# RWKV chunks as affine maps of the state

## The chip, the cores and the metric

The kernel runs on one core of one Trainium2 chip. The metric is the device time of one execution in microseconds (us), lower is better. A core has a matrix engine (TensorE, PE in the views, with its weight loads as PEld), a vector engine (VectorE, DVE), a scalar engine (ScalarE, ACT), GpSimd (POOL) and SyncE (SP), which issues transfers. Each engine works through its own list of instructions in order and waits at an instruction until what that needs is there.

## What is computed

One inference step of a hybrid layer, for a prompt of 512 tokens and 8 x 4 sample tokens, in fp32. The input projection feeds an HGRN2 branch (a, 4 heads of 128) and an RWKV-7 branch (b, 8 heads of 64); both are projected out, merged by gates and followed by an MLP. The change lies in the RWKV branch of the prompt, whose state S (64 x 64 for each head) goes from token to token:

```python
def step(S, xs):
    rt, wt, kt, vt, kkt, at = xs
    sk = jnp.einsum('bhij,bhj->bhi', S, kkt)
    S = S * wt[:, :, None, :] - sk[..., None] * (kkt * at)[:, :, None, :] + vt[..., None] * kt[:, :, None, :]
    return S, jnp.einsum('bhij,bhj->bhi', S, rt)
...
S, y = lax.scan(step, s0.astype(f32), (tr(r), tr(w), tr(k), tr(v), tr(kk), tr(a)))
...
u = jnp.einsum('btd,dc->btc', h, w_in)
o_a, s_a_new = _hgrn2_branch(u_a, lb, hgrn_norm_w, s_a)
o_b, s_b_new = _rwkv7_branch(u_b, u_b_prev, s_b, ...)
x = x + (gate_a * (o_a @ w_a_out) + gate_b * (o_b @ w_b_out)) @ w_out
x = x + jnp.square(jax.nn.relu(rmsnorm(x) @ w_up)) @ w_down
```

## The kernel before

**GEMM.** Every large product is made of three fp32r products (high x high, low x high, high x low). `split` (L166) takes a loaded weight tile `st` apart: ScalarE writes the high part `whi`, VectorE the rest `wlo`. `in_unit` (L410) makes 128 columns of the input projection in two halves of 24 matmuls, `half_unit` (L1345) the same for the branches' output projections, which come after the recurrences: first branch b, then branch a. `branch` (L1350) loads a branch's output from memory (`ox`) and makes its high and low parts `oh` and `ol`, one pair for each of four heads or head pairs.

**Lanes.** The recurrences are generators. A string `ORDER` lists the units of the input projection and, between them, what is put on either of two lanes; after each unit `pump` takes so many steps from lane X and so many from lane Y, by the rate written in the string (`=25` is 2 of X and 5 of Y). What is not done when the units are through goes on beside the output projection of branch b (`NPB` steps of lane Y for each of its units). Lane X holds both RWKV groups (`rw_all(0)`, `rw_all(1)`) and HGRN head 3 (marked `x`), lane Y the other heads, the state and the sample work; the last one on lane Y is `hg2`, head 2. Lane X has three PSUM banks: two of `pe` and one of `pr`, each handed on when its reader is done. A scheduler of the framework then sets the final order of each engine, and mixes the steps with the GEMM matmuls.

**RWKV.** A group g holds two pairs of heads, and a pair fills the 128 rows. The 512 tokens are 8 chunks of 64. `rw_batch` makes for every chunk the decayed keys and queries (`KR`: part 0 the keys that meet the state, part 1 the queries), and masked products between them (`Az`, `Ar`, from `rw_batch_pa`). `rw_inverse` and `rw_solve` make the inverse matrix `TTp` of every chunk; `rw_values` and `rw_tokens` turn values (`VU`, upper half) and keys (`BE`) round and make `av`. `later_pairs` makes the decays of pairs 2 and 3 and sends them to memory (`sa_d`).

`rw_chain` (L762) then walks the chunks. For each of them TensorE multiplies the state with the keys (`pz`), VectorE makes `z` from it (`ch`, L138, two instructions), TensorE applies the inverse (`pu`, written `rw_chain_pq<-ch,TT`), VectorE copies the result beside the values (`VU`, L788), TensorE makes the new state (`ps`, `rw_chain_pq<-VU,BE`), and VectorE scales it and adds the decayed old one (`st`, L138). The chunk's output `py` is two more products in the same step. So a chunk goes three times from TensorE to VectorE and back. `rw_out` norms the output and turns it round with `swapped` (16 matmuls with the identity, `rw_out_pt`).

Of the kernel before, what the change touches and what calls it, by code (L numbers as in the profile page):

```python
# [60 lines left out]
def hybrid_step(ctx: ExitStack, tc: tile.TileContext, i, o):  # L61
# [438 lines left out]
    bv, zb, Az, Ar, chan, VU, av, BE, yo = ({} for _ in range(9))  # L500
# [25 lines left out]

    def later_pairs():
        for p in (2, 3):
            x = [S(TOK, name="sa") for _ in range(2)]
            decay_and_a(p, *x)  # L530
            for e in range(2):
                nc.sync.dma_start(out=sa_d[:, p - 2, e, :], in_=x[e])
            yield
# [15 lines left out]
    def rw_batch(pairs, xk, xr, xv):  # L549
# [16 lines left out]
        for q, p in enumerate(pairs):  # L566
# [39 lines left out]
            for h in range(2):  # L606
                Az[p, h], Ar[p, h] = (S(512, name="A").rearrange("p (n w) -> p n w", w=64) for _ in range(2))
            for e in range(2):
# [39 lines left out]
    def rw_tokens(p):  # L648
# [6 lines left out]
        for j in range(2):  # L655
            if not e:
                av[g, j] = S(512, name="av").rearrange("p (n e w) -> p n e w", n=4, e=2)
            act(av[g, j][:, :, e, :], pav[:, 4 * j:4 * j + 4, :])
        yield
        for j in range(2):  # L660
# [3 lines left out]
            BE[p, j] = S(512, name="BE").rearrange("p (n h w) -> p n h w", n=4, h=2)  # L664
            act(BE[p, j].rearrange("p n h w -> p (n h w)"), pt)
# [95 lines left out]

    def rw_chain(g):  # L762
# [3 lines left out]
        py_ = pe("rw_chain_py").rearrange("p e (n w) -> p e n w", w=64)  # L766
        ST = {p: S(512, name="st").rearrange("p (n w) -> p n w", w=64) for p in pairs}
        tmp = S(384, name="ch")
        z = tmp[:, 0:256].rearrange("p (e h w) -> p e h w", e=2, h=2)
        dec = tmp[:, 256:384].rearrange("p (e w) -> p e w", e=2)  # L770
        P.memset(z, 0.0)
        for n in range(8):
            pq = pr("rw_chain_pq")
            pz, ps = (pq[:, 128 * j:128 * j + 128].rearrange("p (e w) -> p e w", e=2) for j in range(2))
            pu = pq[64:128, 256:512].rearrange("p (e w) -> p e w", e=2)
            vu = VU[g, n // 2][:, n % 2]
            if n:
                for e, p in enumerate(pairs):
                    for r in hs:
                        mm(pz[r, e, :], KR[p][r, 0, n, :], ST[p][r, n - 1, :])  # L780
            for h, r in enumerate(hs):
                if n:
                    stt(z[r, :, h], pz[r], -1.0, av[g, n // 4][r, n % 4], ALU.mult, ALU.subtract)
                else:
                    tsc(z[r, :, h], av[g, 0][r, 0], -1.0, ALU.mult)
            for e, p in enumerate(pairs):
                mm(pu[:, e], TTp[p][:, n, :], z[:, e].rearrange("p h w -> p (h w)"))
            V.tensor_copy(out=vu[64:128].rearrange("p e h w -> p e (h w)"), in_=pu)  # L788
            for e, p in enumerate(pairs):
                for h, r in enumerate(hs):  # L790
                    mm(ps[r, e, :], BE[p, n // 4][:, n % 4, h, :], vu[:, e, h, :])
            for e, p in enumerate(pairs):
                s = pcs[:, p, n:n + 1]
                if n:
                    stt(ST[p][:, n, :], ps[:, e, :], s, dec[:, e, :], ALU.mult, ALU.add)
                else:
                    tsc(ST[p][:, n, :], ps[:, e, :], s, ALU.mult)
                if n < 7:
                    tsc(dec[:, e, :], ST[p][:, n, :], pcs[:, p, n + 1:n + 2], ALU.mult, 1.0, ALU.mult, eng=P)
            for e, p in enumerate(pairs):  # L800
# [486 lines left out]
    for tok in ORDER.split():  # L1287
# [17 lines left out]
        n = int(n)  # L1305
# [308 lines left out]
```

## Time and profile before

| | |
|---|---|
| median of 3 executions | 1004.47 us (998.51, 1004.47, 1006.31) |
| profiled execution | 998.07 us, of it span 996.4 us |
| TensorE busy | 949.0 us (95%) |
| its weight loads | 900.5 us (90%) |
| VectorE busy | 585.7 us (59%) |
| ScalarE busy | 392.8 us (39%) |
| GpSimd busy | 132.4 us (13%) |
| chain 1 (group 0) / chain 2 (group 1) | 193.9 to 231.9 us / 362.7 to 405.4 us |

The span runs from the first to the last instruction of the profiled execution; 1.67 us of its time lie outside. A matmul's row in the timeline is a group of like matmuls: its start, the time from the first one's start to the last one's end, line, tile written and tiles read, and how many records (an fp32 matmul of small tiles leaves two records, a GEMM matmul one). Matmuls overlap, so the price of a group is read as the distance from its start to the next group's. The number in square brackets at a row's end is the time the engine stood idle before it, with what it waited for.

### The profile page before, as it was taken

Reading aid. Unit: us, or ns where it says so; the run is one execution under the profiler, and the core shown is the slowest. Engines: PE = TensorE matmul, PEld = TensorE weight load, DVE = VectorE, ACT = ScalarE, POOL = GpSimd, SP = SyncE. Lnnn points to the kernel's source line nnn. Section 1 sums busy time; section 2 is a strip of 40 time slices with the busy share of each in tenths; the row PEclk is TensorE's granted clock in tenths of the full one; section 3 lists DMA queues with packets and bytes.
Section 4 is the critical chain, followed back from the end, with each engine's and each line's share of the span. In section 5 each row is a group of like instructions: output and inputs, shape, how many; then the busy total and the mean of one; then the engine's idle time right before and its main releaser. Section 6 shows DMA issues by size and latency. Waiting matters only on the chain.

```text
span 996.4 us, 21381 instructions
## 1 busy us (share of the span) xinstructions
PE 949.0 (95%) x8900; PEld 900.5 (90%) x8900; DVE 585.7 (59%) x1198; ACT 392.8 (39%) x721; POOL 132.4 (13%) x330
## 2 busy tenths in 40 slices
PE   5999998899998899898999999999999999999996
PEld 5999888889987876787899999999999999999995
DVE  6645979578886944698778554444222244445333
ACT  7554545514636431434444333333111233333232
POOL 4486332122222001101000000000000000000000
PEclk9999999999999999999999999999999999999998
DMA  9532343222534132553743642223223332335111
GB/s 265 162 120 85 80 91 98 60 65 81 154 100 107 35 95 65 145 163 121 257 127 121 198 127 84 86 85 86 85 86 90 95 92 85 86 106 144 48 43 48
DMA packets 191091, 106.38 MB, mean 107 GB/s; under 512 B 38945, under 2 KB 179047, under 8 KB 190994
## 3 DMA queue, kind: packets, MB, share of 16 engines
q1 hardware_dynamic: 165424, 95.16, 32.8%
q10 hardware_dynamic: 25570, 9.85, 3.9%
q8 instruction: 70, 1.15, 0.5%
q14 instruction: 27, 0.22, 0.1%
HBM read 85.08 MB, written 18.39 MB: 104 GB/s over the span
## 4 chain that ended last, share of the span: by engine, by line
PE 59%; DVE 4%; DMA 1%; ACT 1%; issue 1%; ACTq 0%; SPq 0%; POOL 0%; DVEq 0%
PE pd L129 24%; PE full_unit_ps L129 19%; PE in_unit_ps L129 7%; PE half_unit_ps L129 4%; PE rw_chain_pq L129 1%; DMA s0A<-in_state_hgrn_dram 1%; PE rw_sample_pn L129 1%; PE rw_chain_py L129 1%; DVE wlo L135 1%; DVE tmp L135 0%; PE fin_t L1468 0%; DVE bn L726 0%; DVE ad L1098 0%; PE hg_head_pl L129 0%; ACT jk L132 0%
## 5 line engine op out<-in xcount | busy, mean ns | idle before, releaser
L132 ACT ACTIVATE whi<-st 128x1024 fp32r<-128x1024 f32 x120 | 126.8, 1057 | 252.6 <-PE pd L129 119.2
L135 DVE TENSOR_TENSOR wlo<-st,whi 128x1024 fp32r<-128x1024 f32 x120 | 148.3, 1236 | 124.8 <-PE full_unit_ps L129 40.3
L129 PE MATMUL in_unit_ps<-h_hi,wlo 128*128 128x272 f32 (+3 forms) x736 | 121.5, 299 | 3.5 <-DVE wlo L135 3.5
L129 PE MATMUL in_unit_ps<-h_hi,whi 128*128 128x272 f32 (+3 forms) x736 | 119.2, 297 | 2.4 <-ACT U L132 1.3
L129 PE MATMUL in_unit_ps<-h_lo,whi 128*128 128x272 f32 (+3 forms) x736 | 120.8, 298 | 0.0
L129 PE MATMUL full_unit_ps<-hd,whi 128*128 128x272 f32 (+2 forms) x832 | 110.2, 288 | 0.0
L129 PEld LDWEIGHTS in_unit_ps<-h_hi,wlo 128*128 128x128 f32 x736 | 103.2, 193 | 7.5 <-DVE wlo L135 4.0
L129 PEld LDWEIGHTS in_unit_ps<-h_hi,whi 128*128 128x128 f32 x736 | 101.8, 191 | 7.6 <-issue 3.5
L129 PEld LDWEIGHTS in_unit_ps<-h_lo,whi 128*128 128x128 f32 x736 | 103.4, 193 | 3.7 <-issue 2.1
L129 PEld LDWEIGHTS full_unit_ps<-hd,whi 128*128 128x128 f32 x832 | 106.4, 188 | 0.0
L129 PE MATMUL pd<-xgl,whi 128*128 128x272 f32 x512 | 70.2, 289 | 0.0
L129 PE MATMUL pd<-xgh,wlo 128*128 128x272 f32 x512 | 69.8, 288 | 0.0
L129 PE MATMUL pd<-xgh,whi 128*128 128x272 f32 x512 | 69.8, 288 | 0.0
L129 PEld LDWEIGHTS pd<-xgl,whi 128*128 128x128 f32 x512 | 66.7, 188 | 0.0
L129 PEld LDWEIGHTS pd<-xgh,whi 128*128 128x128 f32 x512 | 66.2, 188 | 0.0
L129 PEld LDWEIGHTS pd<-xgh,wlo 128*128 128x128 f32 x512 | 66.2, 188 | 0.0
L141 POOL TENSOR_SCALAR ys<-ys,ssf 32x512 f32<-32x512 f32 x1 | 0.8, 831 | 491.1 <-DVE ssf L1497 491.1
L129 PE MATMUL full_unit_ps<-hd,wlo 128*128 128x272 f32 (+2 forms) x416 | 56.8, 288 | 0.0
L129 PEld LDWEIGHTS full_unit_ps<-hd,wlo 128*128 128x128 f32 x416 | 54.0, 188 | 0.0
L135 DVE TENSOR_TENSOR hd<-r,hd 128x544 fp32r<-128x544 f32 x32 | 23.2, 725 | 47.9 <-ACT hd L132 47.9
L135 DVE TENSOR_TENSOR x<-x,full_unit_ps 128x272 f32<-128x272 f32 (+2 forms) x48 | 19.5, 435 | 37.0 <-PE full_unit_ps L129 37.0
L138 DVE SCALAR_TENSOR_TENSOR r<-pd,rsb 128x272 f32<-128x272 f32 x64 | 25.2, 436 | 25.8 <-PE pd L129 23.9
(412 smaller groups left out, 1479.8 us busy)
## 6 DMA issues: line engine op xcount, KB each, us to landing
st<-in_w_in_dram SPq DMA_DIRECT2D x46, 512.0 KB
st<-in_w_up_dram SPq DMA_DIRECT2D x32, 512.0 KB
st<-in_w_down_dram SPq DMA_DIRECT2D x32, 512.0 KB
gt_d<-gt SPq DMA_DIRECT2D x16, 272.0 KB
st<-in_w_out_dram SPq DMA_DIRECT2D x8, 512.0 KB
gtb<-gt_d SPq DMA_DIRECT2D x8, 272.0 KB
gta<-gt_d SPq DMA_DIRECT2D x8, 272.0 KB
x<-xt_d SPq DMA_DIRECT2D x8, 272.0 KB
```

What stands on the lines that cost most here:

```text
L129: T.matmul(out, lhsT, rhs, start=start, stop=stop)
L132: A.activation(out=out, in_=in_, func=func, **kw)
L135: (eng or V).tensor_tensor(out=out, in0=a, in1=b, op=op)
L138: V.scalar_tensor_tensor(out=out, in0=a, scalar=s, in1=b, op0=op0, op1=op1)
L141: (eng or V).tensor_scalar(out=out, in0=a, scalar1=s1, scalar2=s2, op0=op0, op1=op1)
```

## The change

`rw_chain` is written anew, and a step `rw_affine` is put ahead of it. With the chunk's inverse known, the new state is (a matrix of the chunk) times the old state plus a constant of the chunk, and the output likewise. `rw_affine` makes these for each pair and each half of the chunks: `pw`, eight products of `TTp` with `KA` (the turned keys beside what was `av`), copied by ScalarE into `W` and, negated, into `VU`; then `pq`, eight products of `W` with `CB` (what was `BE`, beside what was `Ar`), from which VectorE makes `GQ` in two instructions. The chain then has one group of products per chunk (`VU,CB` and `st,GQ` summed in one PSUM tile) and one VectorE instruction, which scales both pairs. The outputs of all chunks are made after the chain, one pair after the other. `rw_tokens` turns the keys round with 16 more small matmuls per pair (`rw_batch_pk`), and its copies write parts of `KA` and `CB`. `later_pairs` becomes a part of `first_pairs`, so that the decays of pairs 2 and 3 are made early, and their four transfers (on SP's queue) stand between the first loads of `w_in`.

The removed lines of `rw_chain` are those printed above and are left out here.

```diff
--- before.py
+++ after.py
@@ -497,7 +497,7 @@
     zb_d = [dram.tile([4, 16, 32, 32], F32, name=f"zb_d{g}") for g in range(2)]
     xz_d = [dram.tile([4, 16, 32, 32], F32, name=f"xz_d{g}") for g in range(2)]
     gb_d = dram.tile([128, 4, TOK], F32, name="gb_d")
-    bv, zb, Az, Ar, chan, VU, av, BE, yo = ({} for _ in range(9))
+    bv, zb, Az, chan, VU, KA, CB, yo = ({} for _ in range(8))
     zero = S(512, name="zero")
     P.memset(zero, 0.0)
     for g in range(2):
@@ -523,8 +523,6 @@
             sig[p], al[p] = S(TOK, name="sig"), S(TOK, name="al")
             decay_and_a(p, sig[p], al[p])
             yield
-
-    def later_pairs():
         for p in (2, 3):
             x = [S(TOK, name="sa") for _ in range(2)]
             decay_and_a(p, *x)
@@ -604,7 +602,7 @@
             yield
 
             for h in range(2):
-                Az[p, h], Ar[p, h] = (S(512, name="A").rearrange("p (n w) -> p n w", w=64) for _ in range(2))
+                Az[p, h] = S(512, name="A").rearrange("p (n w) -> p n w", w=64)
             for e in range(2):
                 pa = pe("rw_batch_pa")
                 for j in range(4):
@@ -612,9 +610,11 @@
                         r = slice(64 * h, 64 * h + 64)
                         mm(pa[:, h, 128 * j:128 * j + 128], eb[e][r, j], KR[p][r, :, 4 * e + j, :])
                 p4 = pa.rearrange("p h (j m w) -> p h j m w", j=4, m=2)
-                for m, dst in enumerate((Az, Ar)):
-                    for h in range(2):
-                        tt(dst[p, h][:, 4 * e:4 * e + 4, :], p4[:, h, :, m], bc(msk[:, m, :], 1, 4), ALU.mult)
+                for h in range(2):
+
+                    CB[p, e, h] = S(512, name="CB").rearrange("p (n w) -> p n w", n=4)
+                    for m, dst in enumerate((Az[p, h][:, 4 * e:4 * e + 4, :], CB[p, e, h][:, :, 64:128])):
+                        tt(dst, p4[:, h, :, m], bc(msk[:, m, :], 1, 4), ALU.mult)
                 yield
             for k in range(4):
                 (nc.sync, DQ)[k % 2].dma_start(
@@ -653,16 +653,20 @@
             for h in range(2):
                 mm(pav[64 * h:64 * h + 64, n, :], Az[p, h][0:64, n, :], VU[g, n // 2][0:64, n % 2, e, h, :])
         for j in range(2):
-            if not e:
-                av[g, j] = S(512, name="av").rearrange("p (n e w) -> p n e w", n=4, e=2)
-            act(av[g, j][:, :, e, :], pav[:, 4 * j:4 * j + 4, :])
+            KA[p, j] = S(512, name="KA").rearrange("p (n w) -> p n w", n=4)
+            act(KA[p, j][:, :, 64:128], pav[:, 4 * j:4 * j + 4, :])
+        yield
+        pt = LX.one("rw_batch_pk")
+        swapped(KR[p][:, 0].rearrange("p n w -> p (n w)"), pt)
+        for j in range(2):
+            act(KA[p, j][:, :, 0:64], pt[:, 256 * j:256 * j + 256].rearrange("p (n w) -> p n w", n=4))
         yield
         for j in range(2):
             pt = LX.one("rw_batch_pt")
             for n in range(4):
                 T.transpose(pt[:, 128 * n:128 * n + 128], chan[p][j][:, n].rearrange("p m w -> p (m w)"), ident)
-            BE[p, j] = S(512, name="BE").rearrange("p (n h w) -> p n h w", n=4, h=2)
-            act(BE[p, j].rearrange("p n h w -> p (n h w)"), pt)
+            for h in range(2):
+                act(CB[p, j, h][:, :, 0:64], pt.rearrange("p (n h w) -> p n h w", n=4, h=2)[:, :, h])
             yield
 
     TTp, Dg = {}, {}
@@ -759,57 +763,64 @@
             act(TTp[p][64 * c:64 * c + 32, :, 32:64], px[64 * c:64 * c + 32])
         yield
 
+    GQ = {}
+
+    def rw_affine(g):
+
+        for e in range(2):
+            p = 2 * g + e
+            for j in range(2):
+                pw = pe("rw_affine_pw").rearrange("p h (n w) -> p h n w", n=4)
+                for n in range(4):
+                    for h in range(2):
+                        r = slice(64 * h, 64 * h + 64)
+                        mm(pw[64:128, h, n], TTp[p][r, 4 * j + n, :], KA[p, j][r, n, :])
+                W = S(512, name="W1").rearrange("p (h n w) -> p h n w", h=2, n=4)
+                act(W[64:128], pw[64:128, :, :, 0:64])
+                for i2 in range(2):
+                    act(VU[g, 2 * j + i2][64:128, :, e].rearrange("p n h w -> p h n w"),
+                        pw[64:128, :, 2 * i2:2 * i2 + 2, 64:128], AF.Copy, scale=-1.0)
+                yield
+                pq = pr("rw_affine_pq").rearrange("p (n w) -> p n w", n=4)
+                for n in range(4):
+                    for h in range(2):
+                        mm(pq[64 * h:64 * h + 64, n], W[64:128, h, n, :], CB[p, j, h][64:128, n, :])
+                GQ[p, j] = S(512, name="GQ").rearrange("p (n w) -> p n w", n=4)
+                tt(GQ[p, j][:, :, 0:64], bc(I2, 1, 4), pq[:, :, 0:64], ALU.subtract)
+                tt(GQ[p, j][:, :, 64:128], KR[p][:, 1, 4 * j:4 * j + 4, :], pq[:, :, 64:128], ALU.subtract)
+                yield
+
     def rw_chain(g):
 
         pairs = (2 * g, 2 * g + 1)
         hs = (slice(0, 64), slice(64, 128))
...
+        ST = [S(512, name="st").rearrange("p (n e w) -> p n e w", n=4, e=2) for _ in range(2)]
         for n in range(8):
...
+            ps = LX.one("rw_chain_ps")[:, 0:128].rearrange("p (e w) -> p e w", e=2)
             vu = VU[g, n // 2][:, n % 2]
+            for e, p in enumerate(pairs):
+                for h, r in enumerate(hs):
+                    mm(ps[r, e, :], CB[p, n // 4, h][:, n % 4, 0:64], vu[:, e, h, :], e == 0, e == 1 and n == 0)
             if n:
                 for e, p in enumerate(pairs):
                     for r in hs:
...
+                        mm(ps[r, e, :], GQ[p, n // 4][r, n % 4, 0:64], ST[(n - 1) // 4][r, (n - 1) % 4, e, :], False, e == 1)
+            tt(ST[n // 4][:, n % 4], ps, bc(pcs[:, 2 * g:2 * g + 2, n], 2, 64), ALU.mult)
+            yield
+        for e, p in enumerate(pairs):
+            py_ = LX.one("rw_chain_py").rearrange("p (n w) -> p n w", w=64)
+            for n in range(8):
                 for h, r in enumerate(hs):
...
+                    mm(py_[r, n, :], CB[p, n // 4, h][:, n % 4, 64:128], VU[g, n // 2][:, n % 2, e, h, :], True, n == 0)
                 if n:
                     for r in hs:
...
+                        mm(py_[r, n, :], GQ[p, n // 4][r, n % 4, 64:128], ST[(n - 1) // 4][r, (n - 1) % 4, e, :], False, True)
+            yo[p] = S(512, name="yo").rearrange("p (n w) -> p n w", w=64)
+            act(yo[p], py_)
+            yield
+        pw_ = LX.one("rw_chain_pw_")[:, 0:256].rearrange("p (q c) -> p q c", q=2)
         for e, p in enumerate(pairs):
-            yo[p] = S(512, name="yo").rearrange("p (n w) -> p n w", w=64)
-            act(yo[p], py_[:, e])
-        pw_ = pr("rw_chain_pw_")[:, 0:256].rearrange("p (q c) -> p q c", q=2)
-        for e, p in enumerate(pairs):
-            T.transpose(pw_[0:64, e, :], ST[p][:, 7, :], ident)
+            T.transpose(pw_[0:64, e, :], ST[1][:, 3, e, :], ident)
         so = S(256, name="so")
         act(so[0:64], pw_[0:64].rearrange("p q c -> p (q c)"))
         DQ.dma_start(out=o["wkv_p"][0, 0, 4 * g:4 * g + 4].rearrange("h v k -> v h k"),
@@ -983,8 +994,6 @@
             yield from rw_values(g)
             for p in pairs:
                 yield from rw_tokens(p)
-            if g == 0:
-                yield from later_pairs()
 
         more = meanwhile()
         for _ in rw_inverse(g):
@@ -994,6 +1003,7 @@
         yield from more
         for p in pairs:
             yield from rw_solve(p)
+        yield from rw_affine(g)
         yield from rw_chain(g)
         for p in pairs:
             yield from rw_out(p)
```

How the instructions stand on TensorE, at three places. First, one chunk of the second chain. Before, in the program's order (`kr` is KR, `TT` the inverse, `rw_sample` the sample tokens' work):

```order
L129 MATMUL rw_chain_pq_4792<-st_4710,kr_3682 64x64 x2
L129 MATMUL rw_chain_pq_4792<-st_4711,kr_3885 64x64 x2
L129 MATMUL rw_sample_pn_5204<-um_5202,rs_4143 64x512
L129 MATMUL in_unit_ps_5244<-h_hi,whi_5240 128x272 x6
L129 MATMUL rw_chain_pq_4792<-ch_4712,TT_4492 64x128
L129 MATMUL rw_chain_pq_4792<-ch_4712,TT_4653 64x128
L129 MATMUL in_unit_ps_5244<-h_hi,whi_5240 128x272 x2
L129 MATMUL in_unit_ps_5244<-h_hi,wlo_5241 128x272 x3
L968 MATMUL rw_sample_pt_5209<-ident,s0T_3918 128x128 x3
L129 MATMUL rw_chain_pq_4792<-VU_4078,BE_4132 64x64 x2
L129 MATMUL rw_chain_pq_4792<-VU_4078,BE_4285 64x64 x2
```

In the change:

```order
L129 MATMUL rw_chain_ps_5164<-st_5041,GQ_4953 64x64 x2
L129 MATMUL rw_chain_ps_5164<-st_5041,GQ_5037 64x64 x2
L129 MATMUL rw_chain_ps_5174<-VU_4316,CB_3934 64x64
L129 MATMUL rw_chain_ps_5174<-VU_4316,CB_3937 64x64
L129 MATMUL rw_chain_ps_5174<-VU_4316,CB_4167 64x64
L129 MATMUL rw_chain_ps_5174<-VU_4316,CB_4170 64x64
L129 MATMUL in_unit_ps_5513<-h_hi,whi_5484 128x272 x2
L129 MATMUL rw_chain_ps_5174<-st_5041,GQ_4953 64x64 x2
L129 MATMUL rw_chain_ps_5174<-st_5041,GQ_5037 64x64 x2
```

The step with the inverse (`ch,TT`) and the VectorE work on either side of it have gone; two matmuls of the GEMM are left between a chunk's constant part (`VU,CB`) and its state part (`st,GQ`), where 6, 2 and 3 stood between the old steps.

Second, what stands ahead of the second chain. Before, the last rows of `rw_solve` and the first of the chain:

```order
L129 MATMUL rw_solve_py_4670<-XT_4650,zb_4050 32x32 x16
L129 MATMUL in_unit_ps_5169<-h_hi,whi_5140 128x272 x6
L129 MATMUL rw_solve_px_4690<-TT_4653,YT_4687 32x32 x16
L129 MATMUL in_unit_ps_5169<-h_hi,wlo_5141 128x272 x6
L129 MATMUL rw_chain_pq_4714<-ch_4712,TT_4492 64x128
L129 MATMUL rw_chain_pq_4714<-ch_4712,TT_4653 64x128
L129 MATMUL in_unit_ps_5169<-h_hi,wlo_5141 128x272 x2
```

In the change, a part of `rw_affine` that stands between them (eight `pq` per pair and half, of which the rows show the last two and the next first two):

```order
L129 MATMUL rw_affine_pq_4944<-CB_3934,W_4930 64x128
L129 MATMUL rw_affine_pq_4944<-CB_3937,W_4930 64x128
L129 MATMUL rw_affine_pw_4966<-KA_4424,TT_4771 64x128 x8
L129 MATMUL in_unit_ps_5320<-h_lo,whi_5291 128x272 x5
L129 MATMUL in_unit_ps_5488<-h_hi,whi_5484 128x272 x2
L129 MATMUL rw_affine_pq_5003<-CB_4140,W_4975 64x128
L129 MATMUL rw_affine_pq_5003<-CB_4143,W_4975 64x128
```

These are new rows: 32 `pw` and 32 `pq` for each group, in runs of eight or sixteen between runs of the GEMM.

Third, the end of the second lane against the start of branch a's output projection. `hg_head_pt<-ident,hy` are head 2's last transposes, `half_unit_ps` the output projections; the `oh` of the first rows are branch b's, and those behind the line of dots branch a's, the third of which (`oh_6902` before, `oh_7064` in the change) is head 2's. Before:

```order
L1161 MATMUL hg_head_pt_6669<-ident,hy_6647 128x128 x4
L129 MATMUL half_unit_ps_6797<-ol_6415,whi_6747 128x272
L129 MATMUL half_unit_ps_6821<-oh_6396,whi_6815 128x272
...
L129 MATMUL half_unit_ps_6865<-ol_6415,whi_6815 128x272
L129 MATMUL half_unit_ps_6920<-oh_6890,whi_6914 128x272
L129 MATMUL half_unit_ps_6920<-oh_6896,whi_6914 128x272
L129 MATMUL half_unit_ps_6933<-oh_6890,whi_6914 128x272
L129 MATMUL half_unit_ps_6920<-oh_6902,whi_6914 128x272
```

In the change:

```order
L1171 MATMUL hg_head_pt_6831<-ident,hy_6809 128x128 x4
L129 MATMUL half_unit_ps_7014<-ol_6577,whi_6977 128x272
L129 MATMUL half_unit_ps_7027<-oh_6558,whi_6977 128x272
...
L129 MATMUL half_unit_ps_7027<-ol_6577,whi_6977 128x272
L129 MATMUL half_unit_ps_7082<-oh_7052,whi_7076 128x272
L129 MATMUL half_unit_ps_7095<-oh_7052,whi_7076 128x272
L129 MATMUL half_unit_ps_7117<-oh_7052,whi_7076 128x272
L129 MATMUL half_unit_ps_7082<-oh_7058,whi_7076 128x272
L129 MATMUL half_unit_ps_7082<-oh_7064,whi_7076 128x272
```

Between the transposes and the first row that reads head 2's `oh` stand 55 rows of `half_unit` before, and 19 in the change: four blocks of twelve of branch b's have become one.

## Rows read from the trace of the kernel before

**Rows 1.** The page's busy time, share of the span and instructions of each engine.

```profile
PE 949.0 (95%) x8900; PEld 900.5 (90%) x8900; DVE 585.7 (59%) x1198; ACT 392.8 (39%) x721; POOL 132.4 (13%) x330
```

**Rows 2.** Table of stretches: us; then busy us (instructions) per engine; TensorE clock, DMA share, GB/s.

```profile
194.00:232.00 38.00, 38.00 (x493) 30.87 (x495) 26.30 (x75) 8.03 (x21) 7.47 (x19) 1.00 0.14 45
362.00:405.00 43.00, 42.99 (x406) 29.78 (x405) 20.45 (x56) 6.94 (x15) 5.24 (x16) 1.00 0.23 57
405.00:486.00 81.00, 74.00 (x892) 66.85 (x889) 67.02 (x173) 34.21 (x75) 5.74 (x15) 0.98 0.54 166
486.00:530.00 44.00, 41.33 (x441) 38.88 (x442) 32.12 (x69) 17.23 (x34) 1.53 (x5) 1.00 0.55 180
```

**Rows 3.** VectorE instructions on the chain's tile: ns min/median/max, first and last start, forms.

```profile
L138 DVE SCALAR_TENSOR_TENSOR ch<-rw_chain_pq,av x28: 274/288/296, 197.3 to 401.4; 64x128 f32<-64x128 f32 x28
L138 DVE SCALAR_TENSOR_TENSOR st<-rw_chain_pq,pcs,ch x28: 274/280/285, 200.1 to 404.1; 128x64 f32<-128x64 f32 x28
L788 DVE COPY VU<-rw_chain_pq x16: 427/428/428, 194.6 to 402.6; 64x256 f32<-64x256 f32 x16
```

**Rows 4.** Timeline of TensorE, one chunk of chain 1: start us, us, engine, line, operation.

```profile
198.10 0.65 PE L129 MATMUL rw_chain_pq<-ch,TT 128*64 128x128 f32 x4
198.68 0.90 PE L129 MATMUL in_unit_ps<-h_hi,wlo 128*128 128x276 f32 x5
199.51 0.45 PE L129 MATMUL rw_chain_pq<-VU,BE 128*64 128x64 f32 x8
199.79 0.29 PE L129 MATMUL rw_chain_py<-VU,A 128*64 128x64 f32 x4
...
201.25 0.45 PE L129 MATMUL rw_chain_pq<-st,kr 64*64 64x64 f32 x8
201.62 0.90 PE L129 MATMUL in_unit_ps<-h_lo,whi 128*128 128x276 f32 x5
```

**Rows 5.** Timeline of TensorE, GEMM of a later stage with nothing between.

```profile
618.02 2.19 PE L129 MATMUL pd<-xgl,whi 128*128 128x272 f32 x16
620.05 2.17 PE L129 MATMUL pd<-xgh,whi 128*128 128x272 f32 x16
```

**Rows 6.** Timeline of TensorE: swapped products of rw_out, products of rw_batch.

```profile
245.03 1.15 PE L129 MATMUL rw_out_pt<-ident,yo 64*64 64x64 f32 x32
246.11 0.45 PE L129 MATMUL hg_head_pu<-X 128*32 128x32 f32 x16
...
305.90 1.16 PE L129 MATMUL rw_batch_pa<-kr,eb 64*128 64x128 f32 x16
306.99 0.65 PE L129 MATMUL in_unit_ps<-h_hi,wlo 128*128 128x272 f32 x3
```

**Rows 7.** Timeline of TensorE at its longest wait there, and the stretches behind it.

```profile
456.50 0.52 PE L129 MATMUL in_unit_ps<-h_hi,wlo 128*128 128x272 f32 x2 [3.39 <-DVE wlo L135]
...
456.00:460.00 4.00, 3.08 (x27) 2.64 (x27) 4.00 (x10) 1.75 (x5) 1.99 (x5) 0.75 0.45 135
460.00:464.00 4.00, 4.00 (x31) 3.84 (x31) 4.00 (x6) 2.05 (x6) 0.10 (x1) 0.83 0.40 131
```

**Rows 8.** Timelines at the start of branch a's output projection: TensorE, VectorE, ScalarE.

```profile
513.86 0.65 PE L1161 MATMUL hg_head_pt<-ident,hy 128*128 128x128 f32 x4
514.86 0.74 DVE L138 SCALAR_TENSOR_TENSOR hog<-hg_head_pt,prm,xq 128x512 f32<-128x512 f32 x1
...
520.71 1.06 ACT L132 ACTIVATE whi<-st 128x1024 fp32r<-128x1024 f32 x1 [3.49 <-PE half_unit_ps L129]
521.67 1.19 ACT L132 ACTIVATE oh<-ox 128x544 fp32r<-128x544 f32 x2
521.83 0.93 PE L129 MATMUL half_unit_ps<-oh,whi 128*128 128x272 f32 x3 [0.67 <-DVE mb L138]
```

**Rows 9.** Nearest copies out of PSUM: ScalarE's av, VectorE's A (columns as in rows 3).

```profile
L132 ACT ACTIVATE av<-rw_batch_pav x8: 363/380/395, 157.7 to 328.7; 128x256 f32<-128x256 f32 x8
L135 DVE TENSOR_TENSOR A<-rw_batch_pa,msk x32: 360/415/426, 116.2 to 312.9; 128x256 f32<-128x256 f32 x32
```

More of the change, by code (lines that the diff above doesn't have):

```diff
@@ L765, in rw_chain @@
         hs = (slice(0, 64), slice(64, 128))
[L766 to L771, printed above, removed]
+        ST = [S(512, name="st").rearrange("p (n e w) -> p n e w", n=4, e=2) for _ in range(2)]
         for n in range(8):
-            pq = pr("rw_chain_pq")
-            pz, ps = (pq[:, 128 * j:128 * j + 128].rearrange("p (e w) -> p e w", e=2) for j in range(2))
-            pu = pq[64:128, 256:512].rearrange("p (e w) -> p e w", e=2)
+            ps = LX.one("rw_chain_ps")[:, 0:128].rearrange("p (e w) -> p e w", e=2)
             vu = VU[g, n // 2][:, n % 2]
+            for e, p in enumerate(pairs):
+                for h, r in enumerate(hs):
+                    mm(ps[r, e, :], CB[p, n // 4, h][:, n % 4, 0:64], vu[:, e, h, :], e == 0, e == 1 and n == 0)
             if n:
@@ L779, in rw_chain @@
                     for r in hs:
[L780 to L785, printed above, removed]
-            for e, p in enumerate(pairs):
-                mm(pu[:, e], TTp[p][:, n, :], z[:, e].rearrange("p h w -> p (h w)"))
-            V.tensor_copy(out=vu[64:128].rearrange("p e h w -> p e (h w)"), in_=pu)
@@ L789, in rw_chain @@
-            for e, p in enumerate(pairs):
-                for h, r in enumerate(hs):
[L791 to L799, printed above, removed]
@@ L800, in rw_chain @@
-            for e, p in enumerate(pairs):
-                for h, r in enumerate(hs):
-                    mm(py_[r, e, n, :], Ar[p, h][:, n, :], vu[:, e, h, :], True, n == 0)
+                        mm(ps[r, e, :], GQ[p, n // 4][r, n % 4, 0:64], ST[(n - 1) // 4][r, (n - 1) % 4, e, :], False, e == 1)
[4 more added lines that the diff above has]
+            for n in range(8):
+                for h, r in enumerate(hs):
+                    mm(py_[r, n, :], CB[p, n // 4, h][:, n % 4, 64:128], VU[g, n // 2][:, n % 2, e, h, :], True, n == 0)
@@ L803, in rw_chain @@
                 if n:
                     for r in hs:
-                        mm(py_[r, e, n, :], KR[p][r, 1, n, :], ST[p][r, n - 1, :], False, True)
+                        mm(py_[r, n, :], GQ[p, n // 4][r, n % 4, 64:128], ST[(n - 1) // 4][r, (n - 1) % 4, e, :], False, True)
+            yo[p] = S(512, name="yo").rearrange("p (n w) -> p n w", w=64)
+            act(yo[p], py_)
             yield
+        pw_ = LX.one("rw_chain_pw_")[:, 0:256].rearrange("p (q c) -> p q c", q=2)
         for e, p in enumerate(pairs):
-            yo[p] = S(512, name="yo").rearrange("p (n w) -> p n w", w=64)
@@ L809, in rw_chain @@
-            act(yo[p], py_[:, e])
-        pw_ = pr("rw_chain_pw_")[:, 0:256].rearrange("p (q c) -> p q c", q=2)
-        for e, p in enumerate(pairs):
-            T.transpose(pw_[0:64, e, :], ST[p][:, 7, :], ident)
+            T.transpose(pw_[0:64, e, :], ST[1][:, 3, e, :], ident)
         so = S(256, name="so")
```

## The prediction

> **What bounds the kernel now.** I read the page first. TensorE is busy for 949.0 us of a span of 996.4 [rows 1], so a gain has to come out of TensorE's own work or out of the 47 us in which it stands still. The second view is the table of stretches: the two stretches in which the eight chunks of a group run one after the other are 194 to 232 us and 362 to 405 us, and TensorE is busy for 38.00 of 38.00 and for 42.99 of 43.00 us in them [rows 2]. The third view says why: the chain does make VectorE wait, and its three VectorE steps per chunk (288, 428 and 280 ns, [rows 3]) all lie between two groups of its matmuls, but the timeline of TensorE shows one chunk with GEMM matmuls standing in every gap [rows 4]: 198.68 and 201.62 are GEMM rows between the chain's rows, and no row has idle time in front of it. So the round trips that the change takes out of each chunk are paid by nobody now. Of the time in which TensorE stands still, the part within the change's reach lies behind the second chain: (81 - 74.00) + (44 - 41.33) = 9.7 us between 405 and 530 us [rows 2], of which the longest is a wait of 3.39 us for a weight split of VectorE [rows 7].
>
> **TensorE's work, added and removed.** I take the distance from one group's start to the next, not the rows' own durations, since matmuls overlap.
> - Removed: the product with TT, 16 times. In one chunk it runs from 198.10 to 198.68 [rows 4], 0.58 us for two matmuls of 128 columns (290 ns each): 16 x 0.58 = -9.3 us.
> - Added, pw: 64 matmuls of 64 rows by 128 columns, where the upper and lower half of the rows alternate and write two banks. The nearest row is rw_batch_pa, which alternates in the same manner: eight of them from 305.90 to 306.99 [rows 6], 136 ns each: 64 x 136 ns = +8.7 us.
> - Added, pq: 64 matmuls of the same size, but all read rows 64 to 127 and alternate between the two column halves. The chain's VU,BE alternate between column halves too: four in 0.28 us at 64 columns [rows 4], 70 ns each, or 140 at twice the columns. I take 136 again: +8.7 us. The other bound is TT's 290 ns, at which halves don't overlap: +18.6.
> - Added, pk: the swap of KR for four pairs. The same 16 matmuls for yo run from 245.03 to 246.11 [rows 6]: 4 x 1.08 = +4.3 us.
> - Unchanged in number: the state products (120 of 64 x 64 with GQ where 120 with KR stood) and both output products.
> - Fewer changes between GEMM and small matmuls. In the chunk shown five GEMM matmuls take 198.68 to 199.51, 166 ns each [rows 4]; undisturbed, 16 take 618.02 to 620.05, 127 ns [rows 5]. That is 5 x 39 = 0.2 us for a GEMM run cut at both ends, so about 0.1 per cut. The order of the changed kernel has 168 GEMM runs in the program instead of 175: -0.8 us, with 0 and -1.4 as bounds.
>
> Together -9.3 + 8.7 + 8.7 + 4.3 - 0.8 = **+11.6 us**. This is the firm part: TensorE is the engine that sets the end, and it has more to do. The rule that matters here is in the Trainium skill, TensorEngine Tiling (Array Packing), Key Properties: changing the tiling mode drains TensorE, while different tiles can run in parallel. The trace agrees with its first half by the 166 against 127 ns above. [...]
>
> **What TensorE waits for.**
> - *The chain.* In the second chain of the changed kernel a chunk is four VU,CB, two GEMM matmuls, four st,GQ. Between a chunk's last st,GQ and the next one's first lie four VU,CB (0.28) and two GEMM (0.25 to 0.33), about 0.6 us; they have to cover the matmul's drain and one VectorE step of about 0.28 us (the st row of [rows 3], of the same shape in all but the doubled width). A wait of 0 to 0.2 us per chunk, seven times. The first chain has more GEMM between. The stage of the tokens in the second group gets pk between pav and pt with no GEMM between, and each bank is handed on after two ScalarE copies like av's 380 ns [rows 9]: about 0.6 us per pair. TensorE takes its instructions in order, so the GEMM rows behind a waiting st,GQ or pk wait with it. The two round trips per chunk that go bring nothing, since they were hidden. I take **+1**, with bounds 0 and 4.
> - *The end of branch a.* Head 2's transposes stand at 513.86, VectorE makes hog at 514.86, it goes out to memory and is loaded again, and ScalarE makes oh of it at 521.67; TensorE waits 0.67 us at 521.83 just there [rows 8]. That is 7.8 us from transposes to oh. In the order of before 55 half_unit rows stand between the transposes and the first row that needs head 2's oh; in that of the change 19, since the head comes later in the second lane. 36 rows x 127 ns [rows 5] = **+4.6 us** of cover lost. Bounds: 3.5, as 1.06 us of the 7.8 are a split of ScalarE just ahead of oh [rows 8] that may stand elsewhere, and 6.1, as a wait of this length is followed by a low clock (next).
> - *The wait at 456 us.* TensorE waits 3.39 us for wlo at 456.50, and in the eight microseconds from 456 the granted clock is 0.75 and 0.83 [rows 7], which is (0.25 + 0.17) x 4 = 1.7 us more. VectorE has a pile of sample and head work ahead of that split. In the changed order the sample's and the head's work is spread over more units, and the chain's is over earlier. I take **-3**, with bounds -5.1 (all of it) and 0.
> - *VectorE and ScalarE.* VectorE loses 28 ch, 32 st and 16 copies (28 x 288 + 32 x 280 + 16 x 428 ns = 23.9 us) and gains 16 st and 16 GQ, at some 0.28 to 0.415 us (the A row of [rows 9], the size of GQ) about 11 us: some 13 us less. ScalarE gains about 40 copies of 0.38 us in place of 16, some 15 us. Neither bounds: in the chain's stretches VectorE is busy for 26.30 of 38 us and ScalarE for 8.03 [rows 2]. The masks for CB are the same VectorE work under another name. What is moved to the program's start (the decays of pairs 2 and 3, with their four DMAs on SP's queue between loads of w_in) costs nothing as long as the loads stay ahead; its cost is within the 4 us above.
>
> Sum: 11.6 + 1 + 4.6 - 3 = +14.2 us; from the low bounds 11.6 + 0 + 3.5 - 5.1 = 10.0, from the high ones 11.6 + 4 + 6.1 - 0 = 21.7. The profiled execution took 998.07, so 1012.3 on its footing. It was the fastest of the four shown (998.51, 1004.47 and 1006.31 are the others, mean 1001.8), so I add 3.8 for an ordinary run: **1016 us**. By its own bounds this case is 1012 to 1024.
>
> **Rivals.**
> - *A, not slower: the tail's waits go.* VectorE has some 13 us less to do and the second chain is over sooner, so the splits and heads behind it are no longer late: all 9.7 us of idle time between 405 and 530 us and the 1.7 of low clock vanish. 998.07 + 11.6 - 11.4 = 998.3, with 3.8 some 1002. For it: the waits there are for VectorE. Against it: the head's transposes come later in TensorE's order, and that wait can't vanish. It decides if TensorE's idle time in that stretch falls under 2 us.
> - *B, slower still: pq doesn't overlap.* At 290 ns pq is 64 x 154 ns = 9.9 us dearer: 1026. For it: all pq read the same row half. Against: VU,BE overlap at 70 ns.
> - *C, faster: TensorE is less full than it looks.* In the chains' stretches the weight loads are busy for 30.87 of 38 and 29.78 of 43 us [rows 2]; if the 7.1 + 13.2 = 20.3 us between are slack that the round trips cause, a chain with one round trip gives them back: 998.07 + 11.6 - 20.3 = 989.4, with 3.8 some 993. It decides if the matmuls between chunks are spread rather than packed. Against it: GEMM and chain matmuls follow one another without idle time [rows 4]. The Trainium skill says it this way (Perfetto Trace Analysis, Identifying the Most-Contended Engine): matmul busy time is no good measure of headroom, the share of LDWEIGHTS is; by it the chains' stretches have that room and the time would be the 993, by the rows they don't and it is the 1016.
>
> **How the numbers follow.** Forecast 0.55, A 0.18, B 0.12, C 0.15. This kernel's runs lie 0.8% apart, so within 1% is what can't be told from no change: 994.4 to 1014.5. Three quarters of the forecast's own 1012 to 1024 lie above that: slower 0.55 x 0.75 + 0.12 = 0.53. Of C a third to a half may still be within it, with A whole: same 0.14 + 0.18 + 0.05 = 0.37; faster 0.10. The range runs from 1000 (A in, C out) to 1028 (B in).
>
> **What would show it.** Right: rows of rw_affine_pw and rw_affine_pq at about 1.09 us per eight, pk at 1.08 per 16, GEMM matmuls packed around them; TensorE busy in the profile up by about 11 us; a wait of some 5 us for oh where the first branch-a products start; no wait of 3 us for wlo in the sample's units. Wrong: pq near 290 ns (B); idle time behind the second chain under 2 us (A); GEMM matmuls near 127 ns in the chains' stretches with both stretches shorter by more than their removed matmuls (C).

## The result: 0.5 to 0.7% slower, where 1.4% was forecast

The changed kernel took 1005.81 us (median of 20 executions, 1003.10 to 1010.86) where the kernel before took 1001.14 (20 executions, 995.78 to 1006.31): a ratio of 1.0051, 95% interval 1.0034 to 1.0069. A second comparison, below, gave 1.0070. The forecast was 1016 and 1.4% slower, with 0.53 on slower by over 1%: the way was right, the size was not.

The profiled execution of the changed kernel took 1008.61 us, 10.54 more than the profiled one of before. The page, answering [rows 1]:

```profile
PE 956.8 (95%) x9220; PEld 912.1 (91%) x9220; DVE 574.0 (57%) x1150; ACT 411.5 (41%) x765; POOL 122.4 (12%) x300
```

TensorE has 7.8 us more to do, VectorE 11.7 less, ScalarE 18.7 more. The table of stretches, answering [rows 2] (columns as there): the second chain with its products in bulk, what follows it up to the branches' output projections, and these:

```profile
375.00:402.00 27.00, 27.00 (x376) 21.82 (x374) 7.98 (x21) 7.49 (x19) 0.21 (x1) 1.00 0.14 42
402.00:490.00 88.00, 82.98 (x928) 71.12 (x924) 68.55 (x174) 34.92 (x77) 5.85 (x15) 0.98 0.54 161
490.00:535.00 45.00, 39.97 (x449) 37.13 (x442) 31.69 (x73) 16.64 (x33) 1.54 (x5) 0.90 0.51 167
```

TensorE is full in the chain, as it was before. Behind it, it stands still for 5.0 + 5.0 us, about the 9.7 of before, but at other places, and with a granted clock of 0.90 at the end where it was 1.00.

The timeline of TensorE in the second chain, answering [rows 4]:

```profile
389.02 0.45 PE L129 MATMUL rw_chain_ps<-VU,CB 128*64 128x64 f32 x8
389.40 0.52 PE L129 MATMUL in_unit_ps<-h_lo,whi 128*128 128x272 f32 x2
389.85 0.45 PE L129 MATMUL rw_chain_ps<-st,GQ 64*64 64x64 f32 x8
390.23 0.45 PE L129 MATMUL rw_chain_ps<-VU,CB 128*64 128x64 f32 x8
390.61 0.52 PE L129 MATMUL in_unit_ps<-h_lo,whi 128*128 128x272 f32 x2
```

A chunk takes 1.21 us and nothing waits. Four VU,CB now take 0.38 us, not the 0.28 of [rows 4]: there the output products of the same shape followed, here GEMM does. Two GEMM matmuls take 0.45 where 0.25 would do undisturbed [rows 5].

Where TensorE's time went is in the costliest groups. First the kernel before, then the change (the number behind the bar is busy us):

```profile
L129 PE MATMUL rw_chain_pq<-ch,TT 128*64 128x128 f32 x64 | 10.4, 285 | 0.0
L129 PE MATMUL rw_sample_pn<-um,rs 64*64 64x512 f32 x16 | 8.4, 606 | 0.0
L129 PE MATMUL in_unit_ps<-h_hi,wlo 128*128 128x272 f32 (+3 forms) x736 | 121.5, 299 | 3.5 <-DVE wlo L135 3.5
L129 PE MATMUL in_unit_ps<-h_hi,whi 128*128 128x272 f32 (+3 forms) x736 | 119.2, 297 | 2.4 <-ACT U L132 1.3 <-ACT h_hi L132 1.1
L129 PE MATMUL in_unit_ps<-h_lo,whi 128*128 128x272 f32 (+3 forms) x736 | 120.8, 298 | 0.0
```

```profile
L129 PE MATMUL rw_affine_pw<-KA,TT 64*64 64x128 f32 x128 | 11.1, 275 | 0.0
L129 PE MATMUL rw_affine_pq<-CB,W 64*64 64x128 f32 x128 | 8.7, 276 | 0.0
L129 PE MATMUL rw_batch_pk<-ident,kr 64*64 64x64 f32 x128 | 4.8, 220 | 0.0
L129 PE MATMUL rw_sample_pn<-um,rs 64*64 64x512 f32 x16 | 4.3, 607 | 0.0
L129 PE MATMUL in_unit_ps<-h_hi,wlo 128*128 128x272 f32 (+3 forms) x736 | 116.3, 294 | 0.2 <-DVE wlo L135 0.2
L129 PE MATMUL in_unit_ps<-h_hi,whi 128*128 128x272 f32 (+3 forms) x736 | 120.6, 299 | 4.9 <-ACT xk L132 2.1 <-ACT h_hi L132 1.4 <-ACT U L132 1.3
L129 PE MATMUL in_unit_ps<-h_lo,whi 128*128 128x272 f32 (+3 forms) x736 | 117.7, 295 | 0.0
```

The new products cost what was forecast. But the same sample products (`rw_sample_pn`) went from 8.4 to 4.3 us, which does not stand in the forecast's sum, and the same 2208 matmuls of the input projection went from 361.5 to 354.6, for which the sum had -0.8.

And at the end the late head 2, answering [rows 8]: its transposes, hog, oh, the two waits of TensorE, and the stretch behind them:

```profile
523.35 0.66 PE L1171 MATMUL hg_head_pt<-ident,hy 128*128 128x128 f32 x4
524.04 0.75 DVE L138 SCALAR_TENSOR_TENSOR hog<-hg_head_pt,prm,xq 128x512 f32<-128x512 f32 x1 [0.75 <-PE hg_head_pt L1171]
526.85 1.12 PE L129 MATMUL half_unit_ps<-oh,whi 128*128 128x272 f32 x4 [0.97 <-DVE mb L138]
529.86 1.34 ACT L132 ACTIVATE oh<-ox 128x544 fp32r<-128x544 f32 x2 [2.59 <-DMA ox<-oa_d]
530.57 1.28 PE L129 MATMUL half_unit_ps<-oh,whi 128*128 128x272 f32 x4 [2.60 <-ACT oh L132]
529.00:537.00 8.00, 6.43 (x30) 6.43 (x31) 3.01 (x5) 1.34 (x3) 0.00 (x0) 0.57 0.90 316
```

Here 0.97 + 2.60 us of waiting stand where 0.67 stood, and then eight microseconds with 0.57 of the clock granted, most of them at the lower of its two levels (1.2 for 2.4 GHz): (1 - 0.57) x 8 = 3.4 us of clock, of which TensorE was at work for 2.9; the rest fell into the wait.

### The profile page after: what moved, and what is told of

It is laid out like the page before. It is cut to its first block, busy times and chain, and to the rows that moved or that the text cites. A ratio compares the mean times of both kernels' runs of the same rounds, so it can differ in the third digit from the quotient of the medians.

```text
span 1006.9 us, 21967 instructions
## 1 busy us (share of the span) xinstructions
PE 956.8 (95%) x9220; PEld 912.1 (91%) x9220; DVE 574.0 (57%) x1150; ACT 411.5 (41%) x765; POOL 122.4 (12%) x300
## 4 chain that ended last, share of the span: by engine, by line
PE 70%; DVE 8%; DMA 3%; ACT 2%; issue 1%; POOL 1%; SPq 0%; ACTq 0%; DVEq 0%; POOLq 0%
PE pd L129 24%; PE full_unit_ps L129 19%; PE in_unit_ps L129 13%; PE half_unit_ps L129 4%; DVE tmp L135 2%; PE rw_chain_py L129 2%; DVE wlo L135 1%; PE rw_chain_ps L129 1%; DMA s0A<-in_state_hgrn_dram 1%; PE rw_affine_pw L129 1%; DVE bn L730 1%; PE rw_affine_pq L129 1%; PE hg_head_po L129 1%; DMA ox<-oa_d 1%; ACT L132 1%
## 5 line engine op out<-in xcount | busy, mean ns | idle before, releaser
L129 PE MATMUL in_unit_ps<-h_lo,whi 128*128 128x272 f32 (+3 forms) x736 | 117.7, 295 | 0.0
L129 PE MATMUL in_unit_ps<-h_hi,wlo 128*128 128x272 f32 (+3 forms) x736 | 116.3, 294 | 0.2 <-DVE wlo L135 0.2
L129 PEld LDWEIGHTS in_unit_ps<-h_hi,whi 128*128 128x128 f32 x736 | 101.9, 191 | 10.2 <-issue 3.1
L129 PEld LDWEIGHTS in_unit_ps<-h_hi,wlo 128*128 128x128 f32 x736 | 100.7, 190 | 3.3 <-issue 1.9
```

The lines of the kernel that those rows point to most:

```text
L129: T.matmul(out, lhsT, rhs, start=start, stop=stop)
```

## The experiments

Theory 1 came from these two traces: TensorE's work is the bound all along; the change adds what was forecast, wins back more than was forecast because the rest of its work is cut up less, and pays at the end for a head that comes too late. Theory 2: the profiled execution was an unlucky one, and the missing part of the forecast went into room that TensorE had.

**after_again**, no edit. 

> The changed kernel once more, for a second profile beside the first one, whose 1008.61 us lay above the median of 1005.81. Theory 1 (the late head 2 costs every run): the wait for oh at the first branch-a products is there again at 2.5 to 4 us of idle time, with a granted clock under 0.9 in the eight us behind it, and the time is 1005 +- 3 us. Theory 2 (the first profile was of an unlucky run): the wait is under 1.5 us or the clock behind it is 1.00, and the time is then about 1003 us.

Measured: 1007.97 us, ratio 1.0070 (1.0043 to 1.0097). The waits at the end were 0.97 and 2.38 us again, with a granted clock of 0.79 over 529 to 537 us; a wait of 1.74 us ahead of branch b came again too, with 0.60 behind it. The late end belongs to the kernel.

The record also has the mean granted clock of every execution; one minus that share, times the span, is the time that the clock can have cost. In the mean it is 14.7 us in the change's first 20 executions and 16.9 in these four, and 14.3 to 15.7 in the kernel before (three comparisons, 47 executions). Without it, 991.4 to 991.7 us are left for the change and 984.9 to 986.2 for the kernel before. Below, "lost to the clock" and "the rest" are these two parts.

**head2_earlier**, two edits in the string that sets the order:

```diff
-r2 +rw1 +rs =34 i2 g3 q2 G2 G1 f2 f3 =52 q3 ... G12 G5 G6 G14 =56 +hg2 G0"""
+r2 +rw1 +rs =34 i2 g3 q2 G2 G1 f2 f3 =66 q3 ... G12 G5 +hg2 G6 G14 =56 G0"""
```

> The changed kernel with head 2 of HGRN2 put on its lane two units sooner, and both lanes taking six steps a unit in one stretch; the order then has 59 half_unit rows between head 2's transposes and its first reader instead of 13 (the distance of both in GEMM rows). Theory 1: the idle time (0.97 + 2.60 us) and the low clock behind it (0.57 over eight us, 3.4 us) go from the start of branch a: 4 to 6 us faster than the changed kernel, a ratio to the kernel before of 0.999 to 1.001. Theory 2: under 1.5 us faster.

The 13 rows of the expectation end at branch a's first product; six more, 19, lead to the first that reads head 2's `oh`.

Measured: 997.92 us, ratio 0.9982 (0.9957 to 1.0007): 10 us faster than the four executions of the changed kernel on the same chip, 7 us by the ratio of the first comparison, and no slower than before. TensorE at the start of branch a:

```profile
520.95 1.47 PE L129 MATMUL half_unit_ps<-oh,whi 128*128 128x272 f32 x6 [0.67 <-DVE mb L138]
525.00:535.00 10.00, 10.00 (x82) 10.00 (x81) 8.81 (x16) 4.71 (x7) 0.00 (x0) 1.00 0.19 54
```

The wait is the 0.67 us of [rows 8] again, and the clock stays at 1.00. More was won than the wait and its clock at branch a, so something else went too: 10.7 us are lost to the clock, 4 to 6 us less than in the changed kernel, and the rest is 988.1 us, 3 to 4 us less.

**head2_unit_only** takes the edits apart: only `+hg2` moves, the `=52` stays. 

> The changed kernel with one half of head2_earlier's edit: head 2 joins its lane two units sooner, the lanes' steps per unit stay. Head 2's transposes stand 31 GEMM rows ahead of branch a's first products instead of 13, and the sample work of the other branch ends as late as in the changed kernel. If head 2 at the start of branch a is what costs (Theory 1): most of head2_earlier's gain, 5 to 9 us faster than the changed kernel. If the late sample work at the start of branch b is what costs (1.74 us of idle time and the clock behind it): 0 to 3 us faster.

Measured: 1002.63 us, ratio 1.0026 (1.0006 to 1.0046). So head 2 alone is worth some 2 to 4 us of the 7 to 10 (1.0051 or 1.0070 to 1.0026; the intervals touch, so the share is rough). The other part comes with the `=66`. This kernel still waits 1.73 us for sample work ahead of branch b, and its waits for sample work of over 0.45 us between 440 and 490 us add up to 3.9 us; in head2_earlier they are 1.7, but two waits of 0.60 and 1.02 us at the start of branch b are new there. That leaves 0.6 us less waiting; 2.5 us more of the difference are clock (13.2 us lost here, 10.7 there). That the late sample work is the cause of the other part is not shown.

**before_h2**, the control: both edits in the kernel before. 

> The kernel before with the same edit of the order as head2_earlier, as a control: its head 2 was not late (51 half_unit rows ahead of branch a against 71 now). Theory 1 (the edit only repairs what the change made late): within 3 us of the kernel before. Theory 2 (the edit is worth 8 us by itself): 5 us or more faster, and the affine form is then no better than the old chain in equal order.

Measured: 1000.93 us, ratio 0.9997 (0.9976 to 1.0017). The edit repairs what the change made late; in the old order no gain from it is seen.

**pw_twice** asks if added work is paid. 

> The changed kernel with each of the 64 matmuls pw of rw_affine made twice into the same place: 64 more matmuls of 64 x 128, about 128 ns each in the trace, 8.2 us of TensorE's work. Theory 1 (TensorE is the bound there, work added in rw_affine is on the path): 6 to 10 us slower than the changed kernel; its order has head 2 some 18 GEMM rows sooner, which may take 2 us off. Theory 2 (TensorE has room between the small products, which is where the forecast's 11.6 us went): under 4 us slower.

```diff
-                        mm(pw[64:128, h, n], TTp[p][r, 4 * j + n, :], KA[p, j][r, n, :])
+                        for _ in range(2):
+                            mm(pw[64:128, h, n], TTp[p][r, 4 * j + n, :], KA[p, j][r, n, :])
```

Measured: 1005.62 us, 1.0047 (1.0027 to 1.0067), if anything faster than the changed kernel. That alone would speak for theory 2. But the longer affine step had also moved head 2 up in the order; its waits at branch a were 0.67 and 0.83 us. Only 9.9 us are lost to the clock, 5 to 7 less than in the changed kernel, while the rest is 995.9 us, 4 us more. Two things changed at once, so it was made again on the other order:

**pw_twice_h2.** 

> The kernel of head2_earlier with each of the 64 matmuls pw made twice; head 2's transposes stand at the same place as there, so only the added work differs. Theory 1 (TensorE is the bound in these stretches; in pw_twice the added 7.6 us were paid and the late head 2 no longer): 6 to 9 us slower than head2_earlier, ratio to the kernel before 1.004 to 1.008. Theory 2 (TensorE has room there, the added work hides): under 3 us slower.

Measured: 1007.69 us, ratio 1.0069 (1.0042 to 1.0095), by the ratios 0.87% or 8.7 us above head2_earlier. The products pw in head2_earlier and here:

```profile
L129 PE MATMUL rw_affine_pw<-KA,TT 64*64 64x128 f32 x128 | 11.4, 274 | 0.0
L129 PE MATMUL rw_affine_pw<-KA,TT 64*64 64x128 f32 x256 | 18.9, 272 | 0.0
```

The added ones are busy for 18.9 - 11.4 = 7.5 us. As much is lost to the clock in both kernels (10.7 and 10.6 us), and the rest is 8.5 us more. The intervals leave the 8.7 us some 4 us to either side, which still keeps it clear of no cost. Work added there is paid. Theory 2 falls.

**y_in_chain** puts the output products of each chunk back into the chain's step. 

> The changed kernel with the output products of each chunk made inside the chain again, as before, instead of in bulk after it; the same matmuls, only the place differs. Theory 1 (what the change won back is that the GEMM is cut less and the small products of one shape stand together): 1.5 to 4 us slower than the changed kernel, with GEMM matmuls in the chains' stretches near 160 ns each again. Theory 2 (the order of the small products costs nothing, the gain is in the waits): within 1 us of it.

```diff
             tt(ST[n // 4][:, n % 4], ps, bc(pcs[:, 2 * g:2 * g + 2, n], 2, 64), ALU.mult)
-            yield
-        for e, p in enumerate(pairs):
-            py_ = LX.one("rw_chain_py").rearrange("p (n w) -> p n w", w=64)
-            for n in range(8):
+            for e, p in enumerate(pairs):
...
```

Measured: 1008.85 us, 1.0064 (1.0042 to 1.0087), as the changed kernel; the rest is 991.4 us in both. The products attach to small products that cut the GEMM anyway; in the trace the GEMM has 135 runs between other work from 90 to 560 us where after_again has 137. No gain from the bulk by itself is seen. What could be worth something is the order inside the bulk:

**y_grouped_h2**, on head2_earlier. 

> The kernel of head2_earlier with the 30 output products of a pair put in order of their shape: first the 16 of VU,CB, then the 14 of st,GQ, where now two of the one and two of the other take turns at 0.26 us a turn (15.4 us in all). Theory 1 (each change between a 128 x 64 and a 64 x 64 tile costs about 0.13 us; four of one shape take 0.28): the products take 2.0 to 2.5 us a pair instead of 3.8, 5 to 7 us faster than head2_earlier, ratio to before 0.991 to 0.994. Theory 2 (the price is per matmul): within 1 us of it.

```diff
-                    mm(py_[r, n, :], CB[...], VU[...], True, n == 0)
-                if n:
-                    for r in hs:
-                        mm(py_[r, n, :], GQ[...], ST[...], False, True)
+                    mm(py_[r, n, :], CB[...], VU[...], n == 0, False)
+            for n in range(1, 8):
+                for r in hs:
+                    mm(py_[r, n, :], GQ[...], ST[...], False, n == 7)
```

Measured: 989.85 us, ratio 0.9892 (0.9852 to 0.9933), 8 to 9 us faster than head2_earlier (7 in the repeat below). The timelines of TensorE, of the changed kernel and then of this one:

```profile
396.27 0.45 PE L129 MATMUL rw_chain_py<-VU,CB 128*64 128x64 f32 x8
396.65 0.33 PE L129 MATMUL rw_chain_py<-st,GQ 64*64 64x64 f32 x4
396.91 0.34 PE L129 MATMUL rw_chain_py<-VU,CB 128*64 128x64 f32 x4
397.18 0.33 PE L129 MATMUL rw_chain_py<-st,GQ 64*64 64x64 f32 x4
```

```profile
395.37 1.15 PE L129 MATMUL rw_chain_py<-VU,CB 128*64 128x64 f32 x32
396.45 1.03 PE L129 MATMUL rw_chain_py<-st,GQ 64*64 64x64 f32 x28
397.42 0.41 PE L823 MATMUL rw_chain_pw<-ident,st 128*64 128x128 f32 x2
```

Two st,GQ products (four records) take 0.26 us when the other shape follows, and 14 (28 records) take 0.97 when they stand together, 0.14 for two. Over both groups the output products fall from 19.5 us busy to 9.1, and from 15.2 to 8.2 us by the distance of starts. These 7 us are most of what was won.

**before_y_grouped**, the old chain with its output products put behind it and in the same order. 

> The kernel before with one part of the change alone: the output products of a group after its chain, and in order of shape as in y_grouped_h2; the old chain with its three VectorE steps stays. Theory 1 (fewer changes of shape on TensorE are what the change won): the products take about 9 us instead of 14.6 and the GEMM is cut less in the chain, 4 to 8 us faster than before, 0.992 to 0.996, though the chain's VectorE steps have 5 us less work of its own to hide behind. Theory 2: the three steps per chunk come out of hiding and eat it, within 2 us of before.

Measured: 991.68 us, 0.9908 (0.9874 to 0.9942), 9 us faster than before. The end of the second chain:

```profile
401.33 0.29 PE L129 MATMUL rw_chain_py<-VU,A 128*64 128x64 f32 x4
401.55 1.03 PE L129 MATMUL rw_chain_py<-st,kr 64*64 64x64 f32 x28
402.51 0.41 PE L812 MATMUL rw_chain_pw<-ident,st 128*64 128x128 f32 x2
```

The 14 st,kr of a pair stand in a row as above. The scheduler left the VU,A of one pair in the chain, four records behind each VU,BE, which has their shape. By starts the output products fall from 14.6 to 9.5 us. The expectation's other part, a GEMM that is cut less, did not come: it has 140 runs from 90 to 485 us, as before. What goes beyond the 5 us is in part the clock: 9.9 us are lost to it where the kernel before loses 15.2 in the same comparison. TensorE does not wait in either chain, so the three VectorE steps per chunk stayed hidden. So what was worth having here needs no affine map.

**grouped_affine_again** and **grouped_old_again**, the two on one chip. 

> y_grouped_h2 once more, beside before_y_grouped on the same chip, to tell the two chains apart where both have their output products in order of shape and head 2 at nearly the same place. By the trace the affine form adds 11 us of small products and takes 2 to 5 us of GEMM and 2 us of sample products off, and the waits behind the chain; the two times should be within 3 us: 988 to 992.

> before_y_grouped once more, as the partner of grouped_affine_again: 989 to 994. If it is the faster by over 2 us, the affine form costs more than it brings once the order of shapes is equal; if it is the slower by over 2 us, the affine form pays by itself.

Measured: 991.87 us, 0.9908 (0.9882 to 0.9934), and 992.79 us, 0.9916 (0.9892 to 0.9940). The 0.9 us between them are well inside the noise, which leaves room for some 3.5 us to either side. Shorter chains and a single VectorE step per chunk buy nothing here that TensorE's added products don't take back.

**before_again**, no edit. 

> The kernel before once more, for a second profile: whether the wait of 3.39 us for a weight split at 456 us and the low clock behind it, which the prediction took 3 us for, belong to every run of it. If they do: a wait of 3 to 4 us there, and GEMM plus sample products on TensorE within 2 us of the first profile's. If not, that term was read from one run's accident.

Measured: one execution, 1003.86 us. The wait for wlo was 3.39 us again (3.38 in before_h2), so it is no accident of one run. It is gone in every affine kernel, but also in both runs of the old chain with its output products in order of shape: it hangs on the order of the work, not on the affine form. What differed between the profiles was the clock: summing (1 - granted clock) x 10 over the 10 us stretches up to 600 us, the first profile of before lost 8.5 us, this one 17.0, before_h2 10.2; the changed kernel lost 11.9 and 8.5.

## Why the prediction was wrong in size

The sum was +14.2 us. The medians gave +4.7 and +7.8, the profiled pair 10.5.

- **The small products: right.** By the distance of starts, TT was 9.3 us as forecast, pw and pq 9.6 + 6.9 = 16.5 for 17.4, pk 4.3 for 4.3: +11.5 net. Rival B is out: pq overlaps. Missing were VU,CB, 4.5 to 6.1 us, the output products, 14.6 to 15.2, which lost or changed neighbours of their own shape, and the state products, 5.8 to 5.3: +1.7.
- **"Fewer changes between GEMM and small matmuls", -0.8: the step that failed.** Its row said 0.2 us for a run of GEMM cut at both ends; the prediction halved that and multiplied by seven runs fewer. Measured over the input projection from 90 to 485 us, a GEMM run takes 0.20 us (median) more than 125 ns a matmul when a small tile follows it, 0.11 when another full-array product does. There are 126 runs instead of 140, 8 fewer of the first kind and 6 of the second: 8 x 0.20 + 6 x 0.11 = -2.3. Taken directly, the 2208 matmuls went from 310.1 to 304.9 us by starts; 2.7 of that is clock, which leaves -2.5. The sample products were not in the step at all, though they stood in the order rows shown: as separate rows, with other products between, each half of one takes 1.00 us, and one behind the other they run side by side. The first pair of rows is of before, the second of the change:

```profile
372.94 1.07 PE L129 MATMUL rw_sample_pn<-um,rs 64*64 64x512 f32 x2
373.94 0.65 PE L129 MATMUL rw_chain_pq<-ch,TT 128*64 128x128 f32 x4
```

```profile
406.22 1.07 PE L129 MATMUL rw_sample_pn<-um,rs 64*64 64x512 f32 x4
407.23 1.15 PE L129 MATMUL in_unit_ps<-h_hi,whi 128*128 128x272 f32 x7
```

  One half (two records) takes 1.00 us alone, both (four) take 1.01. By starts that is 7.1 to 4.0 us, -3.1. The Trainium skill (TensorEngine Tiling (Array Packing), Key Properties) says that different tiles can run in parallel; these rows agree. No run moved the sample alone, but the price follows the place: 4.0 us in every kernel that has all four pairs of halves together, 5.0 in head2_earlier, which differs from the change by the order only and has two of the pairs apart. Two smaller groups, `rw_sample_pt` and `rw_batch_pav`, took 1.4 us less. The sum should have read 11.5 + 1.7 - 2.5 - 3.1 - 1.4 = +6.2 where it read +11.6. The page has +7.8, but of the time lost to the clock 8.5 us before and 10.0 after fell into TensorE's busy time, so it is +6.3 at full clock.
- **The chain's own waits, +1: small, as said.** TensorE is busy for 27.00 of 27 us in the second chain. From 90 us to the end of that chain the waits of over 0.45 us add up to 16.5 and 16.3 us in the two profiles of the change, 14.8 and 15.0 in those of before. The largest new one is 2.15 us at 318.58, for a copy of ScalarE's (`xk`).
- **The end of branch a, +4.6 in bounds of 3.5 to 6.1: right.** The wait grew by 2.9 us, and the clock behind it cost 2.9: 5.8 in the first profile. In the second it was 2.7 + 1.7 = 4.4. Not seen at all was the wait of 1.74 us for late sample work ahead of branch b, and the clock behind that.
- **The wait at 456 us, -3 in bounds of -5.1 to 0: it went altogether**, 3.39 us and the clock behind it, as the lower bound had it. But other waits came, for sample loads (1.70 us) and sample work (1.74), so that all the idle time behind the second chain is 10.0 us where it was 9.7. The waits and the clock, +2.6 in the forecast, brought about +4 in the profiled pair.
- **The footing.** The sum was made against a profile that had lost 12.0 us to the clock, and the change's first profile lost 15.1: 3.1 of the pair's 10.5 us. In the means of all executions the two kernels lose alike, 14.3 to 15.7 and 14.7 to 16.9 us, so this part is luck of the pair, and the rest differs by 5 to 7 us, about what TensorE's work at full clock says. The 3.8 us that the prediction added on both sides for an ordinary run do not explain the miss.
- **Rivals.** A did not come: 10.0 us of idle time behind the second chain for 9.7 before. C did not either: chunks were packed and full before and after, and in equal order the two chains take the same time.

## What to carry to other kernels

Where TensorE is full and a chain's round trips hide under other matmuls, shortening the chain bought nothing here; count TensorE's products, and then their neighbours: put products of one tile shape in a row, and let the halves of a split array follow each other. Removing work in one lane of a scheduled program moves the others, so look at the order for what now arrives last ahead of each stage boundary, and price its wait with the clock that falls behind it. The best kernels here owe their gain to neither design but to the order of the 30 output products of each pair: 0.989 and 0.991 of the time before with the affine form (and head 2 earlier), 0.991 and 0.992 with the old chain.

## What the runs showed of the hardware

- Taking turns between 128 x 64 and 64 x 64 tiles cost nearly as much again as the products: two st,GQ took 0.26 us in turns, 0.14 in a row.
- A run of GEMM matmuls took 0.20 us (median) longer than its matmuls at 125 ns each when a small tile followed it.
- A 64 x 512 product on one half of the array took 1.00 us and both halves together 1.01, with nothing between them.
- A wait of 2.6 us of TensorE was followed by eight microseconds at 0.57 of the clock in one execution; in another of the same kernel a wait of 2.4 us was followed by 0.79. The same wait does not have one price.
